# Start addresses of TensorE's operand tiles set to multiples of 512 bytes in a one-core decoder layer

## The chip, the core and the metric

The kernel runs on one core of a Trainium2 chip. The metric is the time of one execution in device microseconds; the listed times of a kernel are the median of its runs with the lowest and the highest. TensorE (PE) multiplies matrices and writes PSUM, VectorE (DVE) and ScalarE (ACT) do element-wise work, GpSimd (POOL) does almost nothing here, and SyncE (SP) issues all DMA transfers. A product of TensorE has two operands in on-chip memory (SBUF): the stationary one is loaded into the array by a weight load (PEld), the moving one is streamed through it column by column.

## What is computed

One layer of a decoder on 256 tokens of width 4096, in float32:

```python
mod = silu(c) @ w_ada + b_ada                    # 4096 x 12288, one row
shift, scale, gate = split(mod, 3)
h = rmsnorm(x, norm_gain) * (1 + scale) + shift
q, k, v, g_attn, u_pool, g_pool = split(h @ w_in)  # 4096 x 12288
y_attn = longnet_mixture(q, k, v) * silu(g_attn)   # 16 heads, 3 dilation patterns
y_pool = multiscale_pool(u_pool, w_pool, pool_scale) * silu(g_pool)
y = concat(y_attn, y_pool) @ w_out                 # 4096 x 4096
out = rmsnorm(x + gate * y, final_gain)
```

Nearly all the work is `h @ w_in`, `y @ w_out`, and the one-row product with `w_ada`, and all three weight matrices are read once.

## The kernel before

**Tiles and products.** Partitions are 128, the contraction is cut into 32 slices of 128 (`KT`), the outputs into chunks of 512 columns (`CH`): 24 chunks of `w_in`, 8 of `w_out`. A piece is two slices of one chunk, 512 KB; SP loads it into one of seven `raw` buffers. `split_piece` (L219) then makes two tiles of it in the type float32r, which TensorE reads in a single pass: ACT casts `raw` into `wh` (L228), DVE subtracts to get the remainder `wl` (L229). There are three buffers of `wh` and three of `wl`. The left operand is split in the same way into `hh` and `hl` (L214, L215). `products` (L232) issues twelve products of 512 columns for each piece (2 slices x 2 halves of the tokens x 3 terms: `wh,hh`, `wh,hl`, `wl,hh`), all from line L239. The moving operand is `wh` or `wl` (128 x 512), the stationary one a 128 x 128 part of `hh` or `hl`; it changes from every product to the next.

**Stages.** In the opening, x is loaded into eight `sb` slots, multiplied with `diag_r` (L325) and kept transposed in `xT`. Up to some 1000 us the one-row product with the first two thirds of `w_ada` runs on DVE (L152, `aacc`) beside the products with `w_in`; after each 256 columns of it `build_h` (L194) makes the next two slices `hh`, `hl`. `visit` (L267) takes the pieces of one chunk that are ready and adds the PSUM result to an accumulator in SBUF (`sa` or `sb`, L280 and L282). From some 1000 to 1235 us the last slices of `w_in` run beside attention (`head`) and pooling (`pool_mix`), whose results go into `yh`, `yl`, which are `sa` slots. Then `out_chunk` (L622) multiplies `yh`, `yl` with the eight chunks of `w_out`, from the same L239; in the last chunk the final six pieces have their split tiles in `sa` slots too (`spare`), and the products of the second half of the tokens are issued last, from L606. The last third of `w_ada` runs on DVE (`gacc`) from some 1000 us on.

**Order.** Everything on an engine runs in the order in which the program issues it. A DMA into a `raw` buffer waits on SP until DVE has read the buffer for `wl` (or for `aacc`, `gacc`), ACT waits before L228 for a free `wh` buffer, which TensorE frees.

**Where tiles lie.** A pool gives each tile a start address in the partition's 224 KB, in steps of 32 bytes, one tile behind the other. The constants come first, so the sizes of small tiles shift all that follow.

Of the kernel before, what the change touches and what calls it, by code (L numbers as in the profile page):

```python
# [46 lines left out]
WLB = 3  # L47
PSB = 2
PSMB = 4
RAW = PIECE * CH  # L50
ADA_COST = 0.728 * PIECE

# [2 lines left out]
def tile_hybrid_block(  # L55
# [22 lines left out]
    strm = ctx.enter_context(tc.tile_pool(name="strm", bufs=2))  # L78

    def slot_a(shape, dtype=F32):  # L80
        return accp.tile(shape, dtype, name="sa", bufs=16)

    def slot_b(shape, dtype=F32):
        return accp.tile(shape, dtype, name="sb", bufs=8)

    ps = ctx.enter_context(tc.tile_pool(name="ps", bufs=PSB, space=PSUM))
    ps_m = ctx.enter_context(tc.tile_pool(name="ps_m", bufs=PSMB, space=PSUM))
# [11 lines left out]
    wo_v = w_out[0].rearrange("(k p) n -> p k n", p=P)  # L99

    ident = const.tile([P, P], F32, name="ident")
    rows = const.tile([P, P], F32, name="rows")
    rows_b = const.tile([P, P], F32, name="rows_b")
    colA = const.tile([P, P], F32, name="colA")
    colB = const.tile([P, 2 * KT], F32, name="colB")
    ones_m = const.tile([P, P], F32, name="ones_m")
    cact = const.tile([P, KT], F32, name="cact")
    ones = const.tile([P, 1], F32, name="ones")
    gb = const.tile([P, KT], F32, name="gb")
    ssq = const.tile([P, NT, 8], F32, name="ssq")  # L110
    rr = const.tile([P, NT], F32, name="rr")
    diag_r = const.tile([P, NT, P], F32, name="diag_r")

    NR = 3 * KT + 16
    nc.sync.dma_start(out=rows[0:KT], in_=c.rearrange("b (k p) -> (b k) p", p=P))
    nc.sync.dma_start(out=ident, in_=k_ident)
    nc.vector.memset(ones, 1.0)
    nc.vector.memset(ones_m, 1.0)
    pt = misc()
    nc.tensor.transpose(out=pt[:, 0:KT], in_=rows[0:KT], identity=ident[0:KT, 0:KT])  # L120
    nc.scalar.activation(out=cact, in_=pt[:, 0:KT], func=AF.Silu)
# [3 lines left out]
    def load_columns():  # L125
        nc.sync.dma_start(out=rows[KT:2 * KT], in_=norm_gain.rearrange("b (k p) -> (b k) p", p=P))
        nc.sync.dma_start(out=rows[3 * KT:NR], in_=pool_scale.rearrange("b (k p) -> (b k) p", p=P))
        nc.sync.dma_start(out=rows_b[0:2 * KT], in_=b_ada.rearrange("b (k p) -> (b k) p", p=P)[0:2 * KT])
        nc.vector.memset(rows[2 * KT:3 * KT], 0.0)
        pt = misc()  # L130
        nc.tensor.transpose(out=pt[:, 0:NR], in_=rows[0:NR], identity=ident[0:NR, 0:NR])
        nc.scalar.copy(out=colA[:, 0:NR], in_=pt[:, 0:NR])
        pt = misc()
        nc.tensor.transpose(out=pt[:, 0:2 * KT], in_=rows_b[0:2 * KT], identity=ident[0:2 * KT, 0:2 * KT])
        nc.vector.tensor_copy(colB, pt[:, 0:2 * KT])
        nc.vector.scalar_tensor_tensor(out=gb, in0=colB[:, KT:2 * KT], scalar=1.0, in1=gainc,
                                       op0=ALU.add, op1=ALU.mult)

# [55 lines left out]
    def build_h(u, acc, pool, xT):  # L194
# [2 lines left out]
        pc = misc()  # L197
        for j in range(2 * uk):
            nc.tensor.matmul(pc[:, j:j + 1], lhsT=acc[:, j * P:(j + 1) * P], rhs=ones, start=True, stop=True)  # L199
        s12 = strm.tile([P, 2, HB], F32, name="s12")  # L200
        ks = slice(k0, k0 + uk)
        nc.vector.tensor_tensor(out=s12[:, 0, 0:uk], in0=pc[:, 0:uk], in1=colB[:, ks], op=ALU.add)
        nc.vector.tensor_tensor(out=s12[:, 1, 0:uk], in0=pc[:, uk:2 * uk], in1=gainc[:, ks], op=ALU.mult)
# [1 line left out]
        for a in range(0, uk, 2):  # L205
            kk = k0 + a
            if kk % HB == 0:
                htile[kk // HB] = [pool.tile([P, HB, S], F32R, name=n) for n in ("hh", "hl")]
            hh, hl = [v[:, kk % HB:kk % HB + 2] for v in htile[kk // HB]]
            hf = strm.tile([P, 2, S], F32, name="hf")  # L210
            for i in range(2):
                nc.scalar.activation(out=hf[:, i], in_=xT[:, kk + i], func=AF.Identity,  # L212
                                     scale=s12[:, 1, a + i:a + i + 1], bias=s12[:, 0, a + i:a + i + 1])
            nc.scalar.copy(out=hh, in_=hf)  # L214
            nc.vector.tensor_tensor(out=hl, in0=hf, in1=hh.bitcast(F32), op=ALU.subtract)  # L215
            for i in range(2):
                hs[kk + i] = (hh[:, i], hl[:, i])

    def split_piece(src, n, spare=False):  # L219
# [3 lines left out]
        if spare:  # L223
            wh, wl = [slot_a([P, PIECE, CH], F32R) for _ in range(2)]
        else:
            wh = strm.tile([P, PIECE, CH], F32R, name="wh", bufs=WHB)
            wl = strm.tile([P, PIECE, CH], F32R, name="wl", bufs=WLB)
        nc.scalar.copy(out=wh[:, 0:n], in_=v[:, 0:n])  # L228
        nc.vector.tensor_tensor(out=wl[:, 0:n], in0=v[:, 0:n], in1=wh[:, 0:n].bitcast(F32), op=ALU.subtract)  # L229
        return wh, wl  # L230
# [59 lines left out]
                b[done]()  # L290
                done += 1

    h_cm = ExitStack()
    ada_cm = ExitStack()
    hp = h_cm.enter_context(tc.tile_pool(name="hp", bufs=WIN, side="right"))
    adap = ada_cm.enter_context(tc.tile_pool(name="ada", bufs=2, side="right"))
    NCH = len(order)
    done = [0] * NCH
    used = [0] * NCH
    with tc.tile_pool(name="xp", bufs=1) as xp:  # L300
        xT = xp.tile([P, KT, S], F32, name="xT")
        first = [ada_tasks(u, adap) for u in range(A0)]
        todo = [f for _, t in first for f in t]
        xs = []
        todo.insert(EARLY, load_columns)

        def load_x(q):
            xs.append(slot_b([P, NT, CH]))
            nc.sync.dma_start(out=xs[q], in_=x_v[:, :, q * CH:(q + 1) * CH])
            for t in range(NT):  # L310
                junk = strm.tile([P, 2, S], F32, name="hf").rearrange("p a s -> p (a s)")
                nc.scalar.activation(out=junk, in_=xs[q][:, t], func=AF.Square, accum_out=ssq[:, t, q:q + 1])

        def r_ready():
            rms_scale(ssq, rr)
            for t in range(NT):
                nc.vector.tensor_scalar(out=diag_r[:, t], in0=ident, scalar1=rr[:, t:t + 1], scalar2=None,  # L317
                                        op0=ALU.mult)

        def flip_x(q):  # L320
            for a in range(2):
                px = misc()
                for i in range(2):
                    for t in range(NT):
                        nc.tensor.matmul(px[:, i * S + t * P:i * S + (t + 1) * P],  # L325
                                         lhsT=xs[q][:, t, (2 * a + i) * P:(2 * a + i + 1) * P], rhs=diag_r[:, t],
                                         start=True, stop=True)
                dst = xT[:, q * 4 + 2 * a:q * 4 + 2 * a + 2].rearrange("p k t -> p (k t)")
                nc.scalar.copy(out=dst, in_=px)  # L329

        nx = 0
        for i, f in enumerate(todo):
            f()
            while i >= EARLY and nx < 8 and (nx + 1) * XSTEP <= (i - EARLY + 1):
                load_x(nx)
                nx += 1
                if nx == 8:
                    r_ready()
                    for q in range(NFLIP):
                        flip_x(q)  # L340
        for u in range(A0):
            build_h(u, first[u][0][0], hp, xT)
        for q in range(NFLIP, 8):
            flip_x(q)

        state = {"ready": A0, "built": A0, "cur": ada_tasks(A0, adap), "credit": 0.0, "age": 0}

        def ada_hook(n):
            st = state
            st["credit"] += n * RATES[min(st["built"], len(RATES) - 1)]  # L350
            st["age"] += 1
            while st["cur"] and st["cur"][1] and st["credit"] > 0:
                if len(st["cur"][1]) == 1 and min(used) < ((US[st["built"] + 1] - 1) // HB - WIN + 1) * HB:
                    st["credit"] = 0.0
                    break
                st["cur"][1].pop(0)()
                st["credit"] -= ADA_COST
            if st["cur"] and not st["cur"][1]:
                u = st["built"]
                build_h(u, st["cur"][0][0], hp, xT)  # L360
                st["built"] += 1
                st["age"] = 0
                st["cur"] = ada_tasks(u + 1, adap) if u + 1 < NU else None
            if st["age"] >= LAG:
                st["ready"] = st["built"]

        hooks.append(ada_hook)
        ptr = 0
        while state["ready"] < NU:
            c = ptr % NCH  # L370
            ptr += 1
            ka, kb = done[c], US[state["ready"]]
            if ka < kb:
                done[c] = kb
                visit(order[c], ka, kb)
                used[c] = kb
            else:
                ada_hook(1.0)
        hooks.remove(ada_hook)
    ada_cm.close()  # L380

    late = ctx.enter_context(tc.tile_pool(name="late", bufs=1, reuse_waits="tile"))

    attc = late.tile([P, 2, 3 * P], F32, name="attc")
    band = late.tile([P, 4, 2 * P + 16], F32, name="band")
# [7 lines left out]
    def transposed(ch, scale):  # L393
        stages = []
        for hf in range(HG // 2):
            def f(hf=hf):
                if hf == 0:
                    qT[ch] = late.tile([P, HG, S], F32, name="tq", bufs=3)
                pt = misc()
                for j in range(2):  # L400
                    hd = hf * 2 + j
# [68 lines left out]
    def pool_mix(g):  # L470
# [3 lines left out]

        def gate_t(a):
            if a == 0:
                k["sg"] = late.tile([P, 4, S], F32, name="tq", bufs=3)
            pt = misc()
            for j in range(2):
                cs = slice((2 * a + j) * P, (2 * a + j + 1) * P)  # L480
# [3 lines left out]

        def band_t(a):
            if a == 0:
                k["ph"] = late.tile([P, 4, S], F32R, name="tq", bufs=3)
                k["pl"] = late.tile([P, 4, S], F32R, name="tq", bufs=3)
            pt = misc()
            for j in range(2):  # L490
                cs = slice((2 * a + j) * P, (2 * a + j + 1) * P)
# [237 lines left out]
```

## Time and profile before

| | |
|---|---|
| time, median of 3 runs | 1597.37 us (1596.73 to 1598.63) |
| span of the profiled execution, first to last instruction | 1594.6 us |
| TensorE busy | 97% of the span, 7043 matmul records |
| VectorE busy | 89% |
| ScalarE busy | 44% |
| moved by DMA | 491 MB, mean 308 GB/s |
| granted TensorE clock, mean | 0.996 of 2.4 GHz |

The profiled execution's span is 2.8 us (0.2%) below the median of the runs. A matmul's recorded duration overlaps with its neighbours', since matmuls are pipelined and their ends are modelled; the time that a product costs is read from start to start, or from a row of the chain of waits that gives a stretch's length and its number of products. The program splits a product of plain float32 into two records; one in float32r is one record.

### The profile page before, as it was taken

What the parts mean: (1) busy time and instruction counts of PE and PEld (TensorE: products, weight loads), DVE (VectorE), ACT (ScalarE), POOL (GpSimd) and SP (SyncE); (2) the same over time, 40 slices, a digit from 0 to 9 for tenths busy, and PEclk for the clock granted to TensorE, in tenths of its full rate; (3) what the DMA queues carried; (4) which work ended last, traced back from release to release, by engine and by line L of the source; (5) the groups of instructions that cost most, each with busy time, mean ns of one, the idle gap of its engine ahead of it and who ended that gap; (6) DMA issues with size and microseconds to landing.
All of it is one profiled execution on the core that took longest, in us unless ns stands there. A gap on an engine that the chain in (4) does not pass through costs nothing.

```text
span 1594.6 us, 20360 instructions
## 1 busy us (share of the span) xinstructions
PE 1546.9 (97%) x7043; PEld 1258.4 (79%) x7043; DVE 1411.8 (89%) x1759; ACT 697.5 (44%) x820; POOL 0.7 (0%) x5
## 2 busy tenths in 40 slices
PE   3999999999999999999999999999999999999997
PEld 2777788888888888888888888888888888888775
DVE  5888998999999998899999988989988788898886
ACT  4655343343443434344344343556554434443343
POOL 0000000000000000000000000000000000000000
PEclk9999999999999999999999999999999999999998
DMA  9999999999999999999999998977678899998886
GB/s 330 365 323 354 315 322 308 313 300 330 317 306 309 310 319 299 309 315 326 340 320 316 325 322 295 311 234 238 212 247 268 287 360 332 314 332 319 323 305 251
DMA packets 324087, 491.11 MB, mean 308 GB/s; under 512 B 19320, under 2 KB 150664, under 8 KB 323984
## 3 DMA queue, kind: packets, MB, share of 16 engines
q1 hardware_dynamic: 323984, 489.82, 91.2%
q8 instruction: 55, 0.90, 0.2%
q14 instruction: 48, 0.39, 0.1%
HBM read 485.55 MB, written 4.19 MB: 307 GB/s over the span
## 4 chain that ended last, share of the span: by engine, by line
PE 90%; DMA 4%; DVE 4%; issue 1%; ACT 1%; SPq 0%; DVEq 0%; ACTq 0%
PE mm L239 82%; DVE aacc L152 2%; DMA raw<-in_w_ada_dram 1%; PE psm L606 1%; DMA raw<-in_w_in_dram 1%; DVE wl L229 1%; PE psm L239 1%; PE psm L199 1%; DMA raw<-in_w_out_dram 1%; DMA sb<-in_x_dram 1%; ACT wh L228 0%; PE psm L427 0%; PE psm L403 0%; PE psm L557 0%; PE psm L514 0%
## 5 line engine op out<-in xcount | busy, mean ns | idle before, releaser
L228 ACT CAST wh<-raw 128x1024 fp32r<-128x1024 f32 x514 | 538.1, 1050 | 729.3 <-PE mm L239 569.6
L229 DVE TENSOR_TENSOR wl<-raw,wh 128x1024 fp32r<-128x1024 f32 x514 | 625.9, 1221 | 55.8 <-ACT wh L228 47.6
L239 PE MATMUL mm<-wh,hh 128*128 128x512 f32 x1536 | 617.3, 402 | 4.2 <-ACT wh L228 4.2
L239 PE MATMUL mm<-wh,hl 128*128 128x512 f32 x1536 | 606.3, 395 | 0.0
L239 PE MATMUL mm<-wl,hh 128*128 128x512 f32 x1536 | 422.7, 396 | 0.6 <-DVE wl L229 0.6
L152 DVE SCALAR_TENSOR_TENSOR aacc<-raw,cact,aacc 128x512 f32<-128x512 f32 x496 | 371.6, 749 | 31.8 <-DMA raw<-in_w_ada_dram 24.5
L239 PEld LDWEIGHTS mm<-wh,hh 128*128 128x128 f32 x1536 | 289.3, 188 | 77.6 <-ACT wh L228 8.1
L239 PEld LDWEIGHTS mm<-wl,hh 128*128 128x128 f32 x1536 | 288.3, 188 | 70.0 <-DVE wl L229 1.0
L239 PEld LDWEIGHTS mm<-wh,hl 128*128 128x128 f32 x1536 | 289.4, 188 | 64.5 <-issue 0.2
L239 PE MATMUL mm<-wh,sa 128*128 128x512 f32 x896 | 225.8, 394 | 1.7 <-ACT wh L228 1.7
L239 PEld LDWEIGHTS mm<-wh,sa 128*128 128x128 f32 x896 | 167.8, 188 | 40.9 <-ACT wh L228 3.3
L152 DVE SCALAR_TENSOR_TENSOR gacc<-raw,cact,gacc 128x512 f32<-128x512 f32 x248 | 185.7, 749 | 13.1 <-DMA raw<-in_w_ada_dram 9.5
L282 DVE TENSOR_TENSOR sa<-mm,sa 128x1024 f32<-128x1024 f32 x92 | 112.5, 1222 | 14.7 <-PE mm L239 14.5
L239 PE MATMUL mm<-wl,sa 128*128 128x512 f32 x448 | 120.9, 392 | 0.3 <-DVE wl L229 0.3
L239 PEld LDWEIGHTS mm<-wl,sa 128*128 128x128 f32 x448 | 84.0, 188 | 19.4 <-DVE wl L229 0.8
L282 DVE TENSOR_TENSOR sb<-mm,sb 128x1024 f32<-128x1024 f32 x48 | 58.7, 1223 | 10.1 <-PE mm L239 10.0
L325 PE MATMUL psm<-diag_r,sb 128*128 128x128 f32 x128 | 16.7, 298 | 16.6 <-DVE diag_r L317 16.6
L325 PEld LDWEIGHTS psm<-diag_r,sb 128*128 128x128 f32 x128 | 16.4, 213 | 16.8 <-DVE diag_r L317 16.8
L212 ACT ACTIVATE hf<-xT,s 128x256 f32<-128x256 f32 x32 | 17.5, 594 | 24.0 <-DVE s L204 23.9
L280 ACT COPY sa<-mm 128x1024 f32<-128x1024 f32 x16 | 16.2, 1015 | 14.4 <-PE mm L239 14.4
L239 PE MATMUL psm<-wh,sa 128*128 128x512 f32 x80 | 20.3, 396 | 0.5 <-ACT wh L228 0.5
L199 PEld LDWEIGHTS psm<-ones,aacc 128*128 128x128 f32 x128 | 16.7, 191 | 2.9 <-ACT xT L329 1.6
(113 smaller groups left out, 617.0 us busy)
## 6 DMA issues: line engine op xcount, KB each, us to landing
raw<-in_w_in_dram SPq DMA_DIRECT2D x384, 512.0 KB, 5.5
raw<-in_w_ada_dram SPq DMA_DIRECT2D x512, 256.0 KB, 5.2
raw<-in_w_ada_dram SPq DMA_DIRECT2D x128, 512.0 KB, 6.4
raw<-in_w_out_dram SPq DMA_DIRECT2D x128, 512.0 KB, 7.0
sb<-in_x_dram SPq DMA_DIRECT2D x16, 512.0 KB, 6.3
raw<-in_w_pool_dram SPq DMA_DIRECT2D x8, 512.0 KB, 4.7
out_dram<-sb SPq DMA_DIRECT2D x16, 256.0 KB, 2.8
fg<-in_final_gain_dram SPq DMA_DIRECT2D x8, 256.0 KB, 4.9
```

The source lines that it names most:

```text
L152: nc.vector.scalar_tensor_tensor(out=acc, in0=r, scalar=cact[:, kt:kt + 1], in1=init if kt == 0 else acc, op0=ALU.mult, op1=ALU.add)
L199: nc.tensor.matmul(pc[:, j:j + 1], lhsT=acc[:, j * P:(j + 1) * P], rhs=ones, start=True, stop=True)
L212: nc.scalar.activation(out=hf[:, i], in_=xT[:, kk + i], func=AF.Identity, scale=s12[:, 1, a + i:a + i + 1], bias=s12[:, 0, a + i:a + i + 1])
L228: nc.scalar.copy(out=wh[:, 0:n], in_=v[:, 0:n])
L229: nc.vector.tensor_tensor(out=wl[:, 0:n], in0=v[:, 0:n], in1=wh[:, 0:n].bitcast(F32), op=ALU.subtract)
L239: nc.tensor.matmul(pt[t], lhsT=hv[i][p][:, t * P:(t + 1) * P], rhs=w[:, i], start=started, stop=ended)
L280: nc.scalar.copy(out=accs[ch], in_=pt)
L282: nc.vector.tensor_tensor(out=accs[ch], in0=pt, in1=accs[ch], op=ALU.add)
L325: nc.tensor.matmul(px[:, i * S + t * P:i * S + (t + 1) * P], lhsT=xs[q][:, t, (2 * a + i) * P:(2 * a + i + 1) * P], rhs=diag_r[:, t], star ...
L606: nc.tensor.matmul(pt[t], lhsT=h[:, t * P:(t + 1) * P], rhs=w, start=False, stop=last and e == len(seq) - 1)
```

## The change

Two things are done.

First, tiles that TensorE reads in a product get a start address that is a multiple of 512 (`align_bytes=LINE`): `sa`, `sb`, `hh`, `hl`, `wh`, `wl` and the three `tq` buffers of attention and pooling. This table gives the start addresses in the two built programs, modulo 512; a slice of such a tile that TensorE reads starts a multiple of 512 bytes behind it, so the table holds for every product.

| tile | used as | before | after |
|---|---|---|---|
| `wh`, `wl` (three buffers each) | moving in L239; stationary in the pooling's L514 to L516 | 416 | 0 |
| `hh`, `hl` (five buffers each) | stationary in L239 up to 1213 us | 480 | 0 |
| `sa` (16 slots; `yh`, `yl`, accumulators, spare split tiles) | stationary in L239 from 1213 us on; moving too in L606 | 352 | 0 |
| `sb` (8 slots) | stationary in L325, moving in the heads' L451 to L453 | 352 | 0 |
| `tq` (three buffers) | moving in L514 to L516, both operands in L426, L427 | 160 | 0 |
| `sm` | stationary in the heads' transposes and L451 to L453 | 160 | 0 |
| `raw` | written by DMA, read by ACT and DVE | 352 | 352 |
| `gacc` | moving in L557 | 416 | 288 |
| `diag_r` | moving in L325 | 256 | 288 |

Second, room is made for the gaps. `rows` and `diag_r`, used in the opening alone, move into the pool `xp` that holds `xT`; `rows_b` loses its own tile and uses `ones_m` for its contents, so that the filling of `ones_m` with ones comes after the transpose that reads it; `s12` moves from the stream pool to the constants. The code of the opening is no longer inside a `with` block, and is otherwise the same.

```diff
+LINE = 512
     def slot_a(shape, dtype=F32):
-        return accp.tile(shape, dtype, name="sa", bufs=16)
+        return accp.tile(shape, dtype, name="sa", bufs=16, align_bytes=LINE)
     def slot_b(shape, dtype=F32):
-        return accp.tile(shape, dtype, name="sb", bufs=8)
+        return accp.tile(shape, dtype, name="sb", bufs=8, align_bytes=LINE)
...
-    rows = const.tile([P, P], F32, name="rows")
-    rows_b = const.tile([P, P], F32, name="rows_b")
     ones_m = const.tile([P, P], F32, name="ones_m")
+    rows_b = ones_m
-    diag_r = const.tile([P, NT, P], F32, name="diag_r")
+    xT = xp.tile([P, KT, S], F32, name="xT")
+    rows = xp.tile([P, P], F32, name="rows")
+    diag_r = xp.tile([P, NT, P], F32, name="diag_r")
...
-    nc.vector.memset(ones_m, 1.0)
     pt = misc()
...
         nc.vector.tensor_copy(colB, pt[:, 0:2 * KT])
+        nc.vector.memset(ones_m, 1.0)
...
-        s12 = strm.tile([P, 2, HB], F32, name="s12")
+        s12 = const.tile([P, 2, HB], F32, name="s12", bufs=2)
...
-                htile[kk // HB] = [pool.tile([P, HB, S], F32R, name=n) for n in ("hh", "hl")]
+                htile[kk // HB] = [pool.tile([P, HB, S], F32R, name=n, align_bytes=LINE) for n in ("hh", "hl")]
...
-            wh = strm.tile([P, PIECE, CH], F32R, name="wh", bufs=WHB)
-            wl = strm.tile([P, PIECE, CH], F32R, name="wl", bufs=WLB)
+            wh = strm.tile([P, PIECE, CH], F32R, name="wh", bufs=WHB, align_bytes=LINE)
+            wl = strm.tile([P, PIECE, CH], F32R, name="wl", bufs=WLB, align_bytes=LINE)
...
+    def wide_tile(dtype):
+        return late.tile([P, HG, S], dtype, name="tq", bufs=3, align_bytes=LINE)
...
-                    qT[ch] = late.tile([P, HG, S], F32, name="tq", bufs=3)
+                    qT[ch] = wide_tile(F32)
```

No instruction is added, dropped or given another shape, and on PE, ACT, POOL and SP the order and the waits stay as they were. One instruction moves, on DVE, in the opening. Before, the memset of `ones_m` stands second:

```order
L117 MEMSET ones 128x1
L118 MEMSET ones_m 128x128
L129 MEMSET rows 32x128
L150 TENSOR_SCALAR aacc<-raw,cact 128x512 [waits DMAHW3_49,DMAHW2_49,Activation_49]
L152 SCALAR_TENSOR_TENSOR aacc<-raw,cact,aacc 128x512 [waits DVE_49]
```

Now it stands between the copy of `colB` (the transposed `rows_b`) and `gb`, and waits for the transfer into its tile:

```order
L161 SCALAR_TENSOR_TENSOR aacc<-raw,cact,aacc 128x512 [waits DVE_49]
L143 COPY colB<-psm 128x64 [waits PE_49]
L144 MEMSET ones_m 128x128 [waits DMAHW4_49]
L145 SCALAR_TENSOR_TENSOR gb<-colB,colA 128x32 [waits DVE_49,Activation_49]
L161 SCALAR_TENSOR_TENSOR aacc<-raw,cact,aacc 128x512 [waits DMAHW3_49,DMAHW2_49]
```

The one row that moved is the memset; the rows around it keep their order.

## Rows read from the trace of the kernel before

**Rows 1.** The page: span, busy time by engine; then the core's granted clock.

```profile
span 1594.6 us, 20360 instructions
PE 1546.9 (97%) x7043; PEld 1258.4 (79%) x7043; DVE 1411.8 (89%) x1759; ACT 697.5 (44%) x820; POOL 0.7 (0%) x5
core 0: 1594.6 us, clock 0.996
```

**Rows 2.** The page: shares of the chain that ended last, by engine, by line.

```profile
PE 90%; DMA 4%; DVE 4%; issue 1%; ACT 1%; SPq 0%; DVEq 0%; ACTq 0%
PE mm L239 82%; DVE aacc L152 2%; DMA raw<-in_w_ada_dram 1%; PE psm L606 1%; DMA raw<-in_w_in_dram 1%; DVE wl L229 1%; PE psm L239 1%; PE psm L199 1%; DMA raw<-in_w_out_dram 1%; DMA sb<-in_x_dram 1%; ACT wh L228 0%; PE psm L427 0%; PE psm L403 0%; PE psm L557 0%; PE psm L514 0%
```

**Rows 3.** Waits of the whole span: in total us, times, longest.

```profile
ACT wh L228 <- PE mm L239: 569.6, 341, 4.4
ACT wh L228 <- DMA raw<-in_w_in_dram: 54.8, 32, 3.9
SPq L222 <- DVE wl L229: 345.5, 283, 5.7
```

**Rows 4.** The chain in order of time: start us, length us, engine, line, number.

```profile
405.49 67.31 PE mm L239 x288
...
1270.57 57.68 PE mm L239 x252
...
1569.42 13.86 PE psm L606 x61
```

**Rows 5.** TensorE in order of time around one `gacc` product: start us, us, operation.

```profile
1067.23 1.02 PE L557 MATMUL psm<-gacc,ones_m 128*128 128x512 f32 x2
1067.68 0.80 PE L239 MATMUL mm<-wh,hh 128*128 128x512 f32 x1
1068.32 0.40 PE L239 MATMUL mm<-wh,hl 128*128 128x512 f32 x1
```

**Rows 6.** TensorE in order of time, pooling: the first and the 46th of a row.

```profile
1193.27 0.28 PE L514 MATMUL psm<-tq,wh 128*128 128x256 f32 x1
...
1198.66 0.28 PE L514 MATMUL psm<-tq,wh 128*128 128x256 f32 x1
```

**Rows 7.** Line L239 alone by stretches: length, busy us (x records) of PE, PEld; clock, DMA.

```profile
0.00:200.00 200.00, 146.63 (x611) 114.91 (x612) 0.99 1.01 337
200.00:1020.00 820.00, 810.82 (x3458) 648.68 (x3457) 1.00 0.95 316
1020.00:1240.00 220.00, 157.87 (x616) 112.31 (x615) 1.00 0.75 241
1240.00:1500.00 260.00, 258.82 (x1121) 210.24 (x1120) 1.00 0.91 321
1500.00:1594.00 94.00, 63.47 (x270) 50.00 (x269) 0.96 0.81 297
```

**Rows 8.** All instructions: length, busy of PE, PEld, DVE, ACT, POOL; clock, DMA share, GB/s.

```profile
0.00:200.00 200.00, 166.31 (x766) 134.57 (x767) 165.96 (x211) 105.06 (x140) 0.20 (x4) 0.99 1.01 337
240.00:960.00 720.00, 720.00 (x3134) 582.01 (x3133) 665.35 (x755) 283.77 (x287) 0.00 (x0) 1.00 0.95 316
720.00:800.00 80.00, 80.00 (x353) 64.78 (x352) 76.07 (x90) 31.39 (x34) 0.00 (x0) 1.00 0.99 335
1020.00:1240.00 220.00, 219.61 (x1228) 184.71 (x1227) 196.56 (x364) 123.55 (x183) 0.00 (x0) 1.00 0.75 241
1240.00:1500.00 260.00, 260.00 (x1129) 211.74 (x1128) 223.74 (x244) 104.90 (x119) 0.00 (x0) 1.00 0.91 321
40.00:80.00 40.00, 36.91 (x185) 30.29 (x183) 35.16 (x45) 27.25 (x33) 0.00 (x0) 1.00 1.07 365
```

**Rows 9.** VectorE in order of time in the opening.

```profile
0.86 0.17 DVE L118 MEMSET ones_m<- 128x128 f32 x1
...
12.55 0.19 DVE L136 SCALAR_TENSOR_TENSOR gb<-colB,colA 128x32 f32<-128x32 f32 x1
19.41 1.54 DVE L152 SCALAR_TENSOR_TENSOR aacc<-raw,cact,aacc 128x512 f32<-128x512 f32 x2 [6.66 <-DMA raw<-in_w_ada_dram]
```

More of the change, by code (lines that the diff above doesn't have):

```diff
@@ L111, in tile_hybrid_block @@
     rr = const.tile([P, NT], F32, name="rr")
-    diag_r = const.tile([P, NT, P], F32, name="diag_r")
+    h_cm = ExitStack()
+    ada_cm = ExitStack()
+    x_cm = ExitStack()
+    hp = h_cm.enter_context(tc.tile_pool(name="hp", bufs=WIN, side="right"))
+    adap = ada_cm.enter_context(tc.tile_pool(name="ada", bufs=2, side="right"))
+    xp = x_cm.enter_context(tc.tile_pool(name="xp", bufs=1))
+    xT = xp.tile([P, KT, S], F32, name="xT")
+    rows = xp.tile([P, P], F32, name="rows")
+    diag_r = xp.tile([P, NT, P], F32, name="diag_r")
     NR = 3 * KT + 16
@@ L291, in merge @@
                 done += 1
[L293 to L296, printed above, removed]
     NCH = len(order)
@@ L299, in tile_hybrid_block @@
     used = [0] * NCH
[L300 to L379, printed above, removed]
@@ new lines, in tile_hybrid_block, with load_x @@
+    first = [ada_tasks(u, adap) for u in range(A0)]
+    todo = [f for _, t in first for f in t]
+    xs = []
+    todo.insert(EARLY, load_columns)
+    def load_x(q):
+        xs.append(slot_b([P, NT, CH]))
+        nc.sync.dma_start(out=xs[q], in_=x_v[:, :, q * CH:(q + 1) * CH])
+        for t in range(NT):
+            junk = strm.tile([P, 2, S], F32, name="hf").rearrange("p a s -> p (a s)")
+            nc.scalar.activation(out=junk, in_=xs[q][:, t], func=AF.Square, accum_out=ssq[:, t, q:q + 1])
@@ new lines, in r_ready, with flip_x @@
+    def r_ready():
+        rms_scale(ssq, rr)
+        for t in range(NT):
+            nc.vector.tensor_scalar(out=diag_r[:, t], in0=ident, scalar1=rr[:, t:t + 1], scalar2=None,
+                                    op0=ALU.mult)
+    def flip_x(q):
+        for a in range(2):
+            px = misc()
+            for i in range(2):
+                for t in range(NT):
+                    nc.tensor.matmul(px[:, i * S + t * P:i * S + (t + 1) * P],
+                                     lhsT=xs[q][:, t, (2 * a + i) * P:(2 * a + i + 1) * P], rhs=diag_r[:, t],
+                                     start=True, stop=True)
+            dst = xT[:, q * 4 + 2 * a:q * 4 + 2 * a + 2].rearrange("p k t -> p (k t)")
+            nc.scalar.copy(out=dst, in_=px)
@@ new lines, in tile_hybrid_block @@
+    nx = 0
+    for i, f in enumerate(todo):
+        f()
+        while i >= EARLY and nx < 8 and (nx + 1) * XSTEP <= (i - EARLY + 1):
+            load_x(nx)
+            nx += 1
+            if nx == 8:
+                r_ready()
+                for q in range(NFLIP):
+                    flip_x(q)
+    for u in range(A0):
+        build_h(u, first[u][0][0], hp, xT)
+    for q in range(NFLIP, 8):
+        flip_x(q)
+    state = {"ready": A0, "built": A0, "cur": ada_tasks(A0, adap), "credit": 0.0, "age": 0}
@@ new lines, in ada_hook @@
+    def ada_hook(n):
+        st = state
+        st["credit"] += n * RATES[min(st["built"], len(RATES) - 1)]
+        st["age"] += 1
+        while st["cur"] and st["cur"][1] and st["credit"] > 0:
+            if len(st["cur"][1]) == 1 and min(used) < ((US[st["built"] + 1] - 1) // HB - WIN + 1) * HB:
+                st["credit"] = 0.0
+                break
+            st["cur"][1].pop(0)()
+            st["credit"] -= ADA_COST
+        if st["cur"] and not st["cur"][1]:
+            u = st["built"]
+            build_h(u, st["cur"][0][0], hp, xT)
+            st["built"] += 1
+            st["age"] = 0
+            st["cur"] = ada_tasks(u + 1, adap) if u + 1 < NU else None
+        if st["age"] >= LAG:
+            st["ready"] = st["built"]
@@ L380, in tile_hybrid_block @@
+    hooks.append(ada_hook)
+    ptr = 0
+    while state["ready"] < NU:
+        c = ptr % NCH
+        ptr += 1
+        ka, kb = done[c], US[state["ready"]]
+        if ka < kb:
+            done[c] = kb
+            visit(order[c], ka, kb)
+            used[c] = kb
+        else:
+            ada_hook(1.0)
+    hooks.remove(ada_hook)
+    x_cm.close()
     ada_cm.close()
     late = ctx.enter_context(tc.tile_pool(name="late", bufs=1, reuse_waits="tile"))
+    def wide_tile(dtype):
+        return late.tile([P, HG, S], dtype, name="tq", bufs=3, align_bytes=LINE)
@@ L476, in gate_t @@
             if a == 0:
-                k["sg"] = late.tile([P, 4, S], F32, name="tq", bufs=3)
+                k["sg"] = wide_tile(F32)
             pt = misc()
@@ L486, in band_t @@
             if a == 0:
-                k["ph"] = late.tile([P, 4, S], F32R, name="tq", bufs=3)
-                k["pl"] = late.tile([P, 4, S], F32R, name="tq", bufs=3)
+                k["ph"] = wide_tile(F32R)
+                k["pl"] = wide_tile(F32R)
             pt = misc()
```

## The prediction, made before the changed kernel ran

> **What bounds the kernel now.** The shares of the span come first: TensorE is busy 97% of 1594.6 us, VectorE 89%, and the clock granted to TensorE is 0.996, the upper of its two levels nearly throughout [rows 1]. Busy TensorE records overlap, so the chain of work that ended last is asked whether TensorE really sets the end: 90% of it is TensorE, and 82% is one line, L239, the twelve products of a piece [rows 2]. The waits agree: ScalarE's cast L228 waits 569.6 us for L239 to free a `wh` buffer and 54.8 us for `w_in` data, so data are mostly there early [rows 3]. Then L239 by stretches: from 200 to 1500 us TensorE hardly stands still, and in 200 to 1020 us alone there are 3458 products of L239 [rows 7]. So the time is a number of products times what one costs from start to start, and any cost per product counts thousands of times.
>
> That cost isn't the same everywhere, although shape, type and line of code are. The chain gives stretches with their counts [rows 4]:
> - stationary at 480 modulo 512, moving at 416 (`hh`, `hl` with `wh`, `wl`): 67.31 us / 288 = 233.7 ns;
> - 352 and 416 (`yh`, `yl` in `sa` with `wh`, `wl`): 57.68 / 252 = 228.9 ns;
> - 352 and 352 (both in `sa`, L606): 13.86 / 61 = 227.2 ns.
>
> How much of that is columns, and how much is the seam between two products? Around a `gacc` product, two records in float32, the next two starts bound it: from 1067.23 to 1068.32 us are 1.09 us, less one L239 product of 0.234 us leaves 0.856 us for four passes over 512 columns, 214 ns each, with hardly a seam [rows 5]. So the seam of an L239 product is about 20, 15 and 13 ns in the three cases. Pooling's 256-column products (stationary 416, moving 160) take 5.39 us / 45 = 119.8 ns [rows 6]; half of 214 is 107, so the seam is 13 ns again. In the two cases with 13 ns both operands sit at the same place modulo 128 (96 and 96; 32 and 32), in the dearer two they don't. After the change they always do, at 0.
>
> **The change part by part.** No instruction changes its shape, and only a memset its place; what can change is the cost of one product.
>
> *L239 on `hh`, `hl`.* I take the seam of the nearest row in which both operands have the same place, L606: 227.2 ns, 6.5 ns less than 233.7. The bounds: no change at all (0 ns), and a vanished seam (214 ns, 19.5 ns less); below nothing comes under the rivals. At 6.5 ns the 3458 products of 200 to 1020 us give 22.5 us; the 616 of 1020 to 1240 us give 4.0 us; of the 611 before 200 us I count half, 2.0 us, since TensorE is idle there 34 of 200 us and waits for data and VectorE [rows 7, 8].
>
> *L239 on `yh`, `yl`.* 228.9 to 227.2 is 1.7 ns: 1121 products to 1500 us give 1.9 us, the 270 after it 0.5 us, of which half, 0.2 us, since the last chunks wait for each other there. L606 is taken as it is.
>
> *Small products* (heads, pooling, transposes) are already at the low seam or too few: 0.
>
> *What is late next.* TensorE's gain is whole only while VectorE keeps up. From 240 to 960 us VectorE is busy 665.35 of 720 us [rows 8]. With products at 227.2 ns that stretch shrinks to 700 us, 95% busy; in its fullest 80 us it now reaches 76.07, which is 95% too [rows 8], so it can be run. The cover ends where 720 us become 665, at 216 ns a product. DMA: 316 GB/s become 325 in that stretch, and 365 was moved from 40 to 80 us [rows 8]; hidden. SP's queue waits for VectorE [rows 3] and moves along.
>
> *The memset of `ones_m`,* 0.17 us [rows 9], now stands on VectorE between `colB` and `gb`. After `gb` VectorE stands idle 6.66 us waiting for `w_ada` [rows 9], so it costs nothing; without that cover 0.2 us. It waits for a transfer that the transpose before it has already waited for. Behind it are queued `gb` and the `aacc` work; `ones_m` itself is first read after 1000 us. `rows`, `diag_r` and `s12` are elsewhere, with the same waits: 0.
>
> Sum: 22.5 + 4.0 + 2.0 + 1.9 + 0.2 = 30.6 us of a span of 1594.6. The median of the runs lies 2.8 us above the span; 1597.4 - 30.6 = 1566.8, say 1567 us.
>
> *A rule against it.* All these addresses, before and after, are multiples of 32, and the three cases still cost 233.7, 228.9 and 227.2 ns [rows 4]. The Trainium skill, SBUF — State Buffer, Specifications (TRN2), gives SBUF lines of 16 bytes, on whose borders every tile lay already; by it nothing changes and the time stays at 1597. The rows do not bear out that such lines are all there is.
>
> **The rivals.**
>
> *The seam shrinks further.* With both starts on a coarse border each read may touch one block less than in any row here, so the 13 ns may fall too. For it: `gacc`'s 214 ns a pass shows columns streaming with no seam to speak of. Against: that was plain float32, with one weight load in two passes, and the two 13 ns cases start at different places and have the same seam, which looks like a floor. At half the seam (220.5 ns) TensorE would want 45 us in 200 to 1020, at none 67 us, but VectorE, at some 97.5% at best (an estimate: 2.5 points over its fullest stretch), allows about 46 us there. With 8 to 12 us from 1020 to 1240, 4 to 6 from the opening, 9 to 16 from 1240 to 1500 and 2 to 3 at the end, the gain is 68 to 83 us: 1514 to 1529 us, and anything between that and the forecast for a seam between. VectorE is then the bound. The Trainium skill, TensorE: Matmul & The Clock Gate, "Wait — 56ns, not 53.3ns?", measures columns / 2.4 GHz + 2.5 ns, 215.7 ns for 512 (in bf16); by it the time would be at the low end, and no L239 row here agrees with it.
>
> *The addresses don't matter.* The three cases differ in more than the start: in which stage they run, and L606 has another sequence of halves. Then the products stay as they are: 1597 us. Against it: the 233.7 ns hold for hundreds of microseconds, through different loads of the other engines.
>
> *Slower: the reads collide.* Weight load and moving stream now begin at the same place modulo 512, and the next weight load begins while the moving operand streams. If that pair is bad instead of good, the seam grows. Price: as far above 233.7 as 227.2 lies below it, 240.2 ns; 3458 x 6.5 = 22.5 us, 616 and 611 products 8 us, and 1391 products at 11.3 ns more 16 us: 1643 us. It decides from a mean product above 233.7 ns in the first stage. Against it: L606 has both operands at the same place modulo 512 and is the cheapest.
>
> **How the numbers follow.** The forecast, with results from 1555 to 1580, has 0.40; a deeper gain, 1512 to 1555, 0.30; a gain of a few microseconds, because only one of the two kinds of pairs improves, 0.06; no change 0.14; slower 0.10. So faster by over 0.2% is 0.76, within 0.2% 0.14, slower 0.10; 0.2%, about 3 us, is what a measurement of this kernel can tell from no change. The range runs from 1512, the floor that VectorE sets, to 1598, no change; it leaves out the slower case and a little at the bottom.
>
> **What would show it.** In the changed kernel's chain, the long stretches of L239 divided by their counts: 227 ns bears out the forecast, 214 to 222 the deeper rival, 234 the third, over 234 the last; the first stage and the `w_out` stage should then have the same value. If TensorE's products are cheap and the time still falls little, VectorE's busy share from 240 to 960 us must be near its end and TensorE must show idle time before L239 with `wh` or `wl` named. The forecast is wrong if the seam depends on something other than where the operands start.

## The result, and the profile after

The changed kernel takes 1567.71 us (median, 1566.17 to 1569.28), the kernel before 1598.0 us beside it; the ratio is 0.9814, 95% interval 0.98 to 0.9829. The forecast was 1567 us.

The page of the changed kernel: span, busy time by engine, shares of the chain that ended last. Its L248 is the old L239, L237 the old L228.

```profile
span 1565.4 us, 20360 instructions
PE 1516.3 (97%) x7043; PEld 1257.5 (80%) x7043; DVE 1405.4 (90%) x1759; ACT 697.6 (45%) x820; POOL 0.7 (0%) x5
PE 91%; DVE 3%; DMA 3%; issue 1%; ACT 1%; SPq 0%; DVEq 0%; ACTq 0%
```

Against [rows 1] the number of instructions is the same, and only TensorE's busy time has changed much: 30.6 us less, with a span 29.2 us shorter. Still TensorE is 91% of the chain. The chain of the changed kernel in order of time (start us, length us), first stage, `w_out` stage and the last products:

```profile
269.45 62.69 PE mm L248 x276
332.93 62.69 PE mm L248 x276
396.41 65.41 PE mm L248 x288
...
1243.35 57.15 PE mm L248 x252
...
1540.58 13.86 PE psm L614 x61
```

Against [rows 4]: 65.41 / 288 = 227.1 ns where there were 233.7, 57.15 / 252 = 226.8 where there were 228.9, and the last row is the same to the digit. All three kinds of pairs now cost the same.

L248 alone by stretches of the changed kernel, cut where about as many products are done as in [rows 7] (length, busy us and records of PE and PEld, clock, DMA share, GB/s):

```profile
200.00:1000.00 800.00, 789.79 (x3462) 648.73 (x3463) 1.00 0.97 324
1000.00:1212.00 212.00, 149.80 (x595) 108.32 (x594) 1.00 0.75 242
1212.00:1470.00 258.00, 256.81 (x1123) 210.35 (x1122) 1.00 0.91 324
```

3458 products took 820 us before, 3462 take 800 now. The first 200 us hold 624 products instead of 611, 13 x 0.23 = 3 us gained in the opening. Part of what TensorE saved but the span didn't is found where the chain of the changed kernel leaves TensorE between 592 and 718 us:

```profile
592.29 62.70 PE mm L248 x276
654.99 0.05 issue
655.04 0.75 DVE aacc L161
655.79 1.15 DVE wl L238
656.94 0.02 issue
656.95 3.94 DMA raw<-in_w_ada_dram
660.90 0.04 issue
660.93 1.23 DVE sa L291
662.16 0.14 issue
662.29 54.71 PE mm L248 x240
```

VectorE waits for a piece of `w_ada`, the addition of a PSUM result into `sa` (L291) is queued behind that on VectorE, and TensorE needs the PSUM tile. The chain is away from TensorE for 7.3 us, from 654.99 to 662.29 us, but that is not how long TensorE stands still: the chain follows what came last, and TensorE meanwhile works on pieces that it already has. Its own rows (start us, us, in brackets the idle time before and what ended it) show the standstill:

```profile
656.63 1.08 PE L248 MATMUL mm<-wl,hh 128*128 128x512 f32 x4
657.54 0.95 PE L208 MATMUL psm<-ones,aacc 128*128 128x1 f32 x8
658.36 0.48 PE L248 MATMUL mm<-wh,hh 128*128 128x512 f32 x1
...
660.27 1.07 PE L248 MATMUL mm<-wl,hh 128*128 128x512 f32 x4
662.29 0.47 PE L248 MATMUL mm<-wh,hh 128*128 128x512 f32 x1 [0.96 <-DVE sa L291]
```

The last of the four products in the row at 660.27 starts at 660.95, the next product at 662.29: 1.34 us where 0.23 are usual, so 1.1 us are lost to a transfer that came too late. Before, TensorE was busy all of 240 to 960 us [rows 8].

### The profile page after: what moved, and what is told of

Same layout as the page of the kernel before. It is cut to its first block, busy times and chain, and to the rows that moved or that the text cites. A ratio compares the mean times of both kernels' runs of the same rounds, so it can differ in the third digit from the quotient of the medians.

```text
span 1565.4 us, 20360 instructions
## 1 busy us (share of the span) xinstructions
PE 1516.3 (97%) x7043; PEld 1257.5 (80%) x7043; DVE 1405.4 (90%) x1759; ACT 697.6 (45%) x820; POOL 0.7 (0%) x5
## 4 chain that ended last, share of the span: by engine, by line
PE 91%; DVE 3%; DMA 3%; issue 1%; ACT 1%; SPq 0%; DVEq 0%; ACTq 0%
PE mm L248 83%; DVE aacc L161 1%; PE psm L614 1%; PE psm L248 1%; DMA raw<-in_w_ada_dram 1%; DMA raw<-in_w_in_dram 1%; PE psm L208 1%; DVE wl L238 1%; ACT wh L237 1%; PE psm L523 0%; PE psm L524 0%; PE psm L522 0%; DMA sb<-in_x_dram 0%; DMA raw<-in_w_out_dram 0%; PE psm L565 0%
## 5 line engine op out<-in xcount | busy, mean ns | idle before, releaser
L237 ACT CAST wh<-raw 128x1024 fp32r<-128x1024 f32 x514 | 538.5, 1050 | 700.0 <-PE mm L248 497.9
L248 PE MATMUL mm<-wh,hh 128*128 128x512 f32 x1536 | 605.4, 394 | 4.8 <-ACT wh L237 3.8
L248 PE MATMUL mm<-wh,hl 128*128 128x512 f32 x1536 | 599.6, 390 | 0.0
L248 PE MATMUL mm<-wl,hh 128*128 128x512 f32 x1536 | 414.2, 391 | 0.6 <-DVE wl L238 0.6
L248 PEld LDWEIGHTS mm<-wh,hh 128*128 128x128 f32 x1536 | 288.8, 188 | 67.0 <-ACT wh L237 7.2
L248 PEld LDWEIGHTS mm<-wl,hh 128*128 128x128 f32 x1536 | 288.4, 188 | 61.1 <-DVE wl L238 1.4
L248 PEld LDWEIGHTS mm<-wh,hl 128*128 128x128 f32 x1536 | 288.9, 188 | 58.3 <-issue 0.2
L248 PE MATMUL mm<-wh,sa 128*128 128x512 f32 x896 | 224.0, 392 | 1.9 <-ACT wh L237 1.9
L248 PEld LDWEIGHTS mm<-wh,sa 128*128 128x128 f32 x896 | 167.7, 188 | 39.7 <-ACT wh L237 3.4
L248 PE MATMUL mm<-wl,sa 128*128 128x512 f32 x448 | 119.8, 389 | 0.0
L291 DVE TENSOR_TENSOR sa<-mm,sa 128x1024 f32<-128x1024 f32 x92 | 112.1, 1218 | 8.5 <-PE mm L248 8.4
L248 PEld LDWEIGHTS mm<-wl,sa 128*128 128x128 f32 x448 | 84.0, 188 | 17.5
L291 DVE TENSOR_TENSOR sb<-mm,sb 128x1024 f32<-128x1024 f32 x48 | 58.5, 1219 | 7.3 <-PE mm L248 7.3
L248 PE MATMUL psm<-wh,sa 128*128 128x512 f32 x80 | 20.1, 394 | 1.4 <-ACT wh L237 1.4
L248 PEld LDWEIGHTS psm<-wh,sa 128*128 128x128 f32 x80 | 14.8, 188 | 5.3 <-ACT wh L237 2.2
```

Of the source, the lines that this page charges most:

```text
L248: nc.tensor.matmul(pt[t], lhsT=hv[i][p][:, t * P:(t + 1) * P], rhs=w[:, i], start=started, stop=ended)
L291: nc.vector.tensor_tensor(out=accs[ch], in0=pt, in1=accs[ch], op=ALU.add)
```

## The experiments

Two theories on the seam stood against each other. **Same place**: a product is cheap when its moving and its stationary operand begin at the same place of a block of 128 bytes. **Border**: it is cheap when they begin on a border, a multiple of 64 or more bytes. Where tiles had to be put on given places, an unused `gap` tile in their pool pushes them.

**hh and hl moved by 64 bytes, in the kernel before.**

```diff
                 htile[kk // HB] = [pool.tile([P, HB, S], F32R, name=n) for n in ("hh", "hl")]
+                if kk == 0:
+                    pool.tile([P, 16], F32, name="gap", bufs=1)
```

> The kernel before, with one edit: hh and hl lie 64 bytes lower, at 416 modulo 512, where wh and wl lie; nothing is aligned to 512. In the w_out stage nothing changes (stationary 352, moving 416). Theory 'same place' (a product's seam is short when both operands begin at the same place modulo 128): long stretches of L239 up to 1000 us fall from 233.7 to 227 ns a product, the w_out stage stays at 229 ns, and the time falls by 22.5 + 4.0 + 2.0 = 28 us to some 1569 us. Theory 'border' (an operand has to begin on a multiple of 64 or more bytes): nothing begins on one, so 233.7 ns and 1598 us stay.

Measured: 1572.96 us, ratio 0.9835 (0.9809 to 0.9861). Its chain:

```profile
396.23 65.45 PE mm L241 x288
...
1246.45 57.68 PE mm L241 x252
```

227.3 ns in the first stage, and 228.9 as in [rows 4] in the `w_out` stage, whose tiles were not touched. Sixteen unused numbers a partition bring most of the gain, with no border anywhere: border falls. The median is 4 us over the expectation. Two of the four runs took 1569 and 1570 us, as expected, two took 1576 us; the profile is of one of the latter. Against the changed kernel's profile, its span is 8.6 us longer: 2.3 us of that are the untouched seam through most of the `w_out` stage, 2.1 us come at the start of that stage and 3.1 us in the last chunks, where TensorE also waits longer for split tiles (1.7 and 4.5 us instead of none and 3.3). The late `w_ada` transfers near 650 and 660 us cost it 1.6 us of standstill, 0.6 more than in the changed kernel.

**The moves without the alignment.**

```diff
-        return accp.tile(shape, dtype, name="sa", bufs=16, align_bytes=LINE)
+        return accp.tile(shape, dtype, name="sa", bufs=16)
...
-                htile[kk // HB] = [pool.tile([P, HB, S], F32R, name=n, align_bytes=LINE) for n in ("hh", "hl")]
+                htile[kk // HB] = [pool.tile([P, HB, S], F32R, name=n) for n in ("hh", "hl")]
```

(`sb`, `wh` and `wl` likewise.)

> The changed kernel without alignment of sa, sb, wh, wl, hh, hl (tq keeps it); the moves of rows, rows_b, diag_r and s12 stay. Tiles then fall where they fall: wh and wl 416, hh and hl 480 as before, sa 416 instead of 352. Same place: first stage unchanged at 233.7 ns; w_out stage, now 416 with 416, at 227 instead of 229 ns: 2 us less, 1596 us, no difference that can be measured. Border: 233.7 and 229 ns, 1598 us. Both: the moved memset and the moved tiles cost nothing.

Measured: 1595.44 us, ratio 0.9978 (0.9968 to 0.9988).

```profile
471.33 67.31 PE mm L248 x288
...
1268.75 57.17 PE mm L248 x252
```

The first stage is as before to the digit. In the `w_out` stage `sa` has fallen to 416 by chance, beside `wh` and `wl`, and 226.9 ns come out; 1391 products by 2 ns are 2.8 us, and the time is 3.0 us lower. The moved memset and tiles themselves cost nothing that can be seen.

**All aligned, but hh and hl at 64.** The kernel without alignment, with a 96-byte gap in the pool of `sa` and a 416-byte gap behind `hl`.

> All operands of L239 begin at 0 modulo 512 as in the changed kernel, but hh and hl at 64. Same place: the distance of 64 bytes is that of the kernel before (416 and 480), so the first stage has 233 to 234 ns and the w_out stage 227 ns, and the time is 1596 us. Border at multiples of 64: 227 ns in both stages and 1567 us. Border at multiples of 128 or more: between the two, the weight load alone off it.

Measured: 1593.93 us, ratio 0.9963 (0.9952 to 0.9975).

```profile
401.47 67.31 PE mm L251 x288
...
1266.10 57.16 PE mm L251 x252
```

Both operands on multiples of 64, and the first stage is back at 233.7 ns, the cost that the same distance of 64 bytes has in the kernel before. The `w_out` stage, all at 0, keeps 226.8.

**All at 416.** The kernel without alignment, with a 64-byte gap behind `hl`.

> The kernel with the moves and without alignment, and hh and hl 64 bytes lower: now wh, wl, hh, hl and sa all begin at 416 modulo 512, none on a multiple of 64. If an equal place is all that counts, both stages have 227 ns a product and the time is that of the changed kernel, 1565 to 1570 us, at no cost in memory. If a border adds anything, it is slower than the changed kernel by over 3 us.

Measured: 1568.73 us, ratio 0.9818 (0.9798 to 0.9838); the changed kernel's interval is 0.98 to 0.9829.

```profile
395.06 65.45 PE mm L250 x288
...
1244.16 57.17 PE mm L250 x252
```

The whole gain, with operands that begin 32 bytes off the nearest multiples of 64. So the alignment works because it puts all operands at one place, not because the place is 0.

**Four distances at a time.** `wh` and `wl` get different places, so each stage has two distances. In the first kernel:

```diff
+    accp.tile([P, 88], F32, name="gap_a", bufs=1)
...
+                strm.tile([P, 64], F32, name="gap_w", bufs=1)
             wh = strm.tile([P, PIECE, CH], F32R, name="wh", bufs=WHB)
+                strm.tile([P, 8], F32, name="gap_l", bufs=1)
             wl = strm.tile([P, PIECE, CH], F32R, name="wl", bufs=WLB)
...
+                    pool.tile([P, 88], F32, name="gap_h", bufs=1)
```

(the gaps within the first use alone; other numbers in the second and third kernel).

> A map in one run: wh at 0, wl at 32, hh and hl at 128, sa at 256 modulo 512. Pairs (moving, stationary): 0 and 128, 32 and 128 in the first stage; 0 and 256, 32 and 256 in the w_out stage. Same place modulo 128: wh products 227 ns in both stages, wl products dearer, 229 to 234 ns. If 0 and 128 are dear, the place counts modulo 256 or 512. Border at 64 or 128: the same split by wh and wl, so this run is for the modulus and the size.

> A map of distances (stationary less moving, modulo 512), wh at 0, wl at 64, hh and hl at 32, sa at 384: 32 and 480 in the first stage, 384 and 320 in the w_out stage. If only an equal place is cheap, all four pairs take 229 to 235 ns, and the time is 1595 to 1603 us. If the cost grows with the distance between two readers, 32 and 480 are nearer to 227 ns than 64 (233.3) and 128 (232.3) were.

> The map goes on: wh at 0, wl at 96, hh and hl at 288, sa at 256: distances 288 and 192 in the first stage, 256 and 160 in the w_out stage. Only an equal place is cheap: all four 229 to 235 ns, 1595 to 1603 us; 256 repeats the 231 ns that it had. A distance under 227 ns here would make a faster kernel than the changed one.

Measured: 1597.21, 1601.69 and 1593.95 us, one run each, beside 1598.45 and 1598.44 us of the kernel before. The chains of the three, in this order:

```profile
403.62 67.04 PE mm L258 x288
...
1266.97 58.49 PE mm L258 x252
```

```profile
405.57 67.31 PE mm L258 x288
...
1271.06 58.53 PE mm L258 x252
```

```profile
399.08 66.55 PE mm L258 x288
...
1262.05 58.52 PE mm L258 x252
```

No stretch is under 231 ns. By pair, as the mean from the start of a product to the start of the next in the trace (left out are the two pairs of the `wl` products in the `w_out` stage of the last two kernels, at 232.2 and 233.6 ns): moving 0 and stationary 128, 232.3 ns; 0 and 256, 231.1 (four_distances) and 231.4 (distances_288); 32 and 128, 232.8; 32 and 256, 234.2; 0 and 32, 232.7; 64 and 32, 233.6; 0 and 384, 232.4; 0 and 288, 232.1; 96 and 288, 228.5. No pair comes down to 227 ns. In the changed kernel the operands lie at different multiples of 512, so being equal modulo 512 is enough. That 128 or 256 bytes apart is not enough is what these means say, with one reservation: each pair shared its stage with another unequal pair, and the next two runs show that a product's time depends on its neighbours. In the `w_out` stage of four_distances, for one, the second of the eight `wh` products of a piece takes 224.6 ns and the fourth 235.3, with the same distance of 256. A kernel with one such distance alone was not run. The nearness of 32 bytes helps nothing.

**wh 16 bytes later.**

```diff
-            wh = strm.tile([P, PIECE, CH], F32R, name="wh", bufs=WHB)
+            wh = strm.tile([P, RAW + 128], F32R, name="wh", bufs=WHB)[:, 4:4 + RAW].rearrange(
+                "p (k n) -> p k n", n=CH)
```

> As the changed kernel, all at 0 modulo 512, but wh begins 16 bytes later; wl at 0. If equality has to be exact, wh products take 229 to 235 ns and wl products 227 ns, some 1585 us. If a block of 32 or more bytes is what counts, wh products stay at 227 ns and the time at 1567 us. If 16 bytes are better than none, under 227 ns.

Measured: 1595.2 us (one run).

```profile
404.50 66.82 PE mm L252 x288
...
1264.16 58.38 PE mm L252 x252
```

232.0 and 231.7 ns: 16 bytes apart is too far already; less was not run. The expectation failed in one point, and with it in the time (1585 us): `wl` products, whose operands are both at 0, also cost 232.0 ns from `wl,hh` to `wl,hh` in this trace, not 227. The four of them follow eight products with a shifted `wh`, so a product's cost depends on those before it too.

**hl alone at 64.** All at 0, a 64-byte gap between the `hh` and `hl` buffers.

> Everything at 0 modulo 512 as in the changed kernel, hl alone at 64. While one product streams its moving tile, the weights of the next product are loaded. Theory 'load against stream' (the cost comes from the place of the next product's stationary tile against the moving tile that streams meanwhile): from a wh,hh product to the following wh,hl product takes long (over 232 ns), from wh,hl to wh,hh takes 227 ns or less, and wl,hh stays at 227 ns. Theory 'own pair' (the place of a product's own two operands counts): the long one is from wh,hl to the next, the short one after wh,hh. Either way about half the loss of the run with both at 64: some 1580 to 1587 us.

Measured: 1578.73 us (one run), a little under the range expected.

```profile
398.64 66.03 PE mm L254 x288
```

229.3 ns, a third of the loss of both at 64, and in neither theory's pattern. The eight `wh` products of a piece repeat in fours; their mean start-to-start times are 226.2 (`hh`), 235.5 (`hl`), 231.6 (`hh`), 227.4 (`hl`). Both theories ask for a pattern of two. The `wl` products have 227.0 to 227.2, so here, unlike in the run before, products with equal places pay nothing beside unequal ones.

That something is carried from product to product shows in the kernel before as well. From 250 to 950 us its twelve products of a piece take 235.9 and 230.9 ns strictly in turn, the four `wl`, `hh` products too, whose pair is the same. In its `w_out` stage 231.4, 226.4 and 228.9 ns follow each other in threes, while `wh`, `yh` and `wh`, `yl` take turns in twos. So the 233.7 and 228.9 ns are means of a pattern in the order of issue, not the price of each product. In the changed kernel the twelve lie between 226.5 and 227.1 ns. What the two readers do to each other, and what is carried on, stays open.

**Eleven products a piece.** To see what comes after the seam, both kernels were run with one of the twelve products of each piece left out.

```diff
         seq += [(t, i, 0, wl) for t in range(NT) for i in range(n)]
+        if n == 2:
+            seq.pop()
```

> The kernel before with the last of the twelve products of each piece left out (one wl,hh product, in both stages): a piece takes TensorE 11 x 233.5 = 2.57 us, as much as twelve products at 214 ns, the columns without any seam. It measures what VectorE and the transfers allow. By the prediction's deeper rival VectorE binds and the time is 1514 to 1529 us. If TensorE still sets the pace, 1485 us. If transfers bind sooner, over 1535 us.

> The changed kernel with the same product left out: 11 x 226.8 = 2.49 us a piece. If VectorE binds already in the run with eleven products of the kernel before, this one is within 10 us of it; if TensorE set the pace there, it is 28 to 32 us faster than it.

Measured: 1541.04 and 1524.79 us, ratios to the kernel before 0.9645 and 0.9543. The waits of the first (us in total, times, longest) and its stretch that answers to 200 to 1020 us (length; PE, PEld, DVE, ACT, POOL; clock, DMA share, GB/s):

```profile
ACT wh L228 <- DMA raw<-in_w_in_dram: 350.5, 230, 5.6
ACT wh L228 <- PE mm L241: 78.4, 57, 4.1
SPq L222 <- DVE wl L229: 239.5, 315, 3.8
200.00:984.00 784.00, 764.40 (x3297) 605.72 (x3296) 751.41 (x859) 326.34 (x334) 0.53 (x1) 1.00 0.98 330
```

In [rows 3] the cast waited 569.6 us for TensorE and 54.8 for `w_in`; now it waits 78.4 for TensorE and 350.5 for `w_in`. In the second kernel it waits 366.0 us for `w_in`. In the stretch shown VectorE is at 95.8%, the DMA share at 0.98. A piece that costs TensorE no more than its columns is thus worth 56 us, not the 68 to 83 that the rival was given, and the second kernel is 16 us faster, about half of what TensorE saves more: neither within 10 us nor 28 to 32, as the two cases of the expectation had it. Transfers and VectorE share that bound; since SP's loads wait for VectorE to free `raw` buffers (239.5 us for L222 in this run), these runs don't separate them.

## Why the prediction was right, and where not

*What bounds the kernel.* Right: the cost of a product counted nearly whole, 29.2 us of span for 30.6 us of TensorE busy time.

*The value taken, 227.2 ns from L606.* Right to 0.4 ns in both stages, and the aligned place brought nothing below it, so the rival of a shrinking seam falls: 13 ns over the 214 of [rows 5] stay when both operands are at the same place, wherever that is (0, 416; 352 in [rows 4]).

*The reason, "the same place modulo 128".* The place is right; the modulus is not borne out: stages with distances of 128 and 256 cost 231 to 233 ns. The step that misled was pooling [rows 6]. Its operands lay 256 apart and were read as a second cheap case; but the 256-column products cost 117 to 121 ns (means by line) at every distance that the runs had, 120 in the changed kernel as before, and say nothing on the seam of 512 columns. The forecast survived since the change makes the places equal modulo 512. That is luck in part: a change that had left them 256 apart would have been given the same forecast.

*The sum.* By the starts of the same products in both traces, up to the 4069th (1020.0 us before, 995.4 us now) 24.5 us were forecast with the opening and 24.6 measured, but not from the same terms. The opening, up to the 611th, gave 3.4 instead of 2.0 us: counting half was too little. From there to the 4069th it is 21.2 instead of 22.5; the products themselves gave the 22.5 (233.3 to 226.8 ns), and 1.1 us went into the late `w_ada` transfer, which the sum held hidden ("365 was moved": a mean rate doesn't show that every piece is in time). From there to the 4685th 2.3 us against 4.0, all 616 products having been counted whole in a stage where L239 was busy for 157.87 of 220 us [rows 7]; which waits took the rest was not followed. From there to the end 2.2 against 2.1. That the total fits to 1.4 us of span comes in part from errors that cancel.

*VectorE as what is late next.* Only half right. At 227 ns there was cover: VectorE is 94% busy in the stretch of the changed kernel that answers to 240 to 960 us, where 95% was forecast (columns as in [rows 8]).

```profile
236.00:942.00 706.00, 705.04 (x3155) 585.11 (x3154) 664.06 (x759) 285.16 (x289) 0.00 (x0) 1.00 0.97 324
```

TensorE lost 0.96 us in it. But the deeper rival's price left the transfers out; eleven products showed them in the waits.

*The memset and the moves.* Nothing, as the kernel with the moves alone shows.

*The other rivals.* That addresses don't matter fell with 64 bytes that brought most of the gain. The two reads do affect each other by where they begin, with the sign turned: in stages with unequal places a product takes 1.4 to 7 ns more on average (228.5 to 234.2 against 227.1). The rule cited ahead of the result, lines of 16 bytes (the Trainium skill, SBUF — State Buffer, Specifications (TRN2)), isn't borne out as the whole: all tiles lay on such lines in every run.

## What to carry to other kernels

When one line of code costs different times per product in different stages, divide the chain's stretches by their counts and compare where the operands begin: a few nanoseconds on thousands of products were 2% here. For float32r products with a new stationary tile each, try moving and stationary operands that begin at the same offset modulo 512 bytes; here an unused gap of 64 bytes a partition brought most of what aligning every tile did, and with all operands at 416 the whole. After such a gain, look for single transfers that have become late, and not at mean rates alone. Where the chain leaves an engine, read that engine's own rows before calling it idle: 7.3 us in the chain were 1.1 us on TensorE.

## What the runs showed of the hardware that was not expected

As the mean of a stage, a float32r product of 512 columns takes 226.8 to 227.3 ns where all operands begin at equal places modulo 512, whatever the place (0, 352, 416), and 228.5 to 234.2 ns by pair otherwise; 16 bytes of difference are enough for 232. A single product's time follows the order of issue too: 235.9 and 230.9 ns in turn with one and the same distance of 64 bytes. A product with equal places beside unequal ones paid in one run (232.0 ns) and not in another (227.0 to 227.2). Plain float32 showed no such seam (214 ns a pass, [rows 5]). Why the seam depends on the difference was not found.
